# 128 bytes of padding ahead of the weight tiles in a two-layer transformer kernel

## The chip, the cores and the metric

The kernel runs on one core of one Trainium2 chip. The metric is the device time of one execution in microseconds (us); a comparison between two kernels is made on the median of several runs.

## The reference

Two layers work on 512 latent tokens and 256 context tokens, 1024 wide, in fp32. Each layer is a half-step SwiGLU, a token mixing (six GQA heads, a short gated convolution and six MLA heads over one input and one output projection), and another half-step SwiGLU. Every sub-layer is scaled, shifted and gated by vectors made from a conditioning vector. Cut to what matters:

```python
def half_ffn(h, g, shift, scale, gate, wg, wu, wd):
    return h + 0.5 * gate * swiglu(modulate(rms_norm(h, g), shift, scale), wg, wu, wd)

for l in range(2):
    ml, mc = silu(c) @ w_mod[l] + b_mod[l], silu(c_ctx) @ w_mod[l] + b_mod[l]   # nine vectors each
    x, ctx = half_ffn(x, ..., wg[l, 0], wu[l, 0], wd[l, 0]), half_ffn(ctx, ...)
    y_l, y_c = token_mixing(modulate(rms_norm(x, ...)), modulate(rms_norm(ctx, ...)), ...)
    x = x + ml[5] * y_l
    x = half_ffn(x, ..., wg[l, 1], wu[l, 1], wd[l, 1])
    if l == 0:                                       # the context isn't needed after the last mixing
        ctx = half_ffn(ctx + mc[5] * y_c, ...)
return x
```

## The kernel before, in words

**Precision.** A weight or an activation in fp32 is split into a high part (a cast to fp32r on ACT) and a low part (a subtraction on DVE), and a product is three matmuls into the same PSUM tile: high weight by high token, high weight by low token, low weight by high token. Each matmul instruction loads its own stationary operand, 128x128, even where the one before had the same (the profile counts 16,088 weight loads, PEld, beside 16,088 matmuls, PE).

```python
def mm3(wh, wl, rh, rl, spans, first, last):
    for st, mv, f, l in ((wh, rh, first, False), (wh, rl, False, False), (wl, rh, False, last)):
        for view, d in spans:
            te.matmul(out=d, lhsT=st, rhs=view(mv), start=f, stop=l)
```

**Stages.** The feed-forward networks take most of the time. Their first chunks of hidden columns are done as plain products (`classical`); the others by seven half-size products in the manner of Strassen (`Tile.p1` to `Tile.p7`), for which DVE makes sums of weights and of tokens. The hidden columns are then multiplied by blocks of the down weights and added to the residual stream. In the mixing stage the projections use tokens as the moving operand where the output is wanted transposed, and tokens as the stationary operand where it is wanted by token: the projection of GQA inputs (`wn`, 384 and 288 columns) and the two up-projections of MLA (`up`, 288 and 384 columns a step). Attention works through units of two blocks of queries.

**Where the order comes from.** The kernel writes the order of the instructions of TensorE (PE), VectorE (DVE) and ScalarE (ACT) by hand in the long stretches (`chain` and `unchain` tie each instruction behind the one before it on its engine); weights come by DMA, nearly all on SP's queue, a buffer or two ahead.

**Where tiles lie.** A tile in SBUF is a byte address, the same in all 128 partitions, and a length. A pool hands out tiles by tag: the first request for a tag sets aside room for all its buffers behind the room that was handed out before, and later requests for that tag reuse it. So the order of first requests sets the addresses. Behind the constants and the residual stream `xT` come, in this order:

| tag | what is in it | bytes of a buffer x buffers | first address modulo 512 |
|---|---|---|---|
| `s` | slots: tokens, activations, split tokens (high and low), attention operands, sometimes split weights | 3072 x 34 | 320 |
| `t` | temporaries, raw down weights of the second half of each network | 3072 x 5 | 320 |
| (small) | small vectors, a few bytes each | | |
| `st`, `st2` | sums of squares, 216 bytes, set aside as 224 | 224 x 1 each | 384, 96 |
| `mscr` | scratch for the largest temporary, raw up weights (`wu`), raw output weights (`wo`) | 4096 x 1 | 320 |
| `ot` | small outputs of attention | 1024 x 2 | 320 |
| `wr` | raw weights as they land from DMA | 4096 x 2 | 320 |
| `wh`, `wl` | high and low parts of a weight block | 4096 x 3 each | 320 |
| `mr` | raw modulation weights; sums of weights (`ws`); some split weights (`we`, `w`) | 4096 x 2 | 320 |
| `mq` | raw modulation weights; gate weights (`wg`) | 4096 x 1 | 320 |

The two tiles `st` and `st2` are requested at one place in the prologue, ahead of the first tile of `mscr`:

```python
    for tag in ("st", "st2"):
        pool.tile([P, NT, 9], F32, name=nm(tag), tag=tag, bufs=1)
    Rs = pool.tile([P, D], F32, name="Rs", tag="mscr", bufs=1)
```

All sizes between a buffer and the next of these tags, and the steps between the blocks of a weight tile (128 columns of 4 bytes) and between the halves of a token tile (384 or 256 columns), are multiples of 512 bytes. So for nearly every matmul the address of the stationary operand and that of the moving operand differ by a multiple of 512. The exceptions are few: in the MLA up-projection of queries the moving weights go in steps of 288 columns, which is 1152 bytes or 128 modulo 512 (tokens are stationary there), and some matmuls have constants (`ident`, `ones`, `sT`, `s4`) as an operand.

In this text the offset of a matmul is the address of its stationary operand minus that of its moving operand, modulo 512.

Of the kernel before, what the change touches and what calls it, by code (L numbers as in the profile page):

```python
# [8 lines left out]
F32 = mybir.dt.float32  # L9
# [6 lines left out]
P = 128  # L16
# [32 lines left out]
def tile_net(ctx: ExitStack, tc: tile.TileContext, a, out):  # L49
# [37 lines left out]
    pool = ctx.enter_context(tc.tile_pool(name="pool", bufs=1))  # L87
# [4 lines left out]
    def nm(s):  # L92
        uid[0] += 1
        return f"{s}{uid[0]}"
# [1981 lines left out]
    wm0_mm(0, 5, KD)  # L2076
    for tag in ("st", "st2"):
        pool.tile([P, NT, 9], F32, name=nm(tag), tag=tag, bufs=1)
    Rs = pool.tile([P, D], F32, name="Rs", tag="mscr", bufs=1)
    se.copy(Rs[:, LAT], Rl)  # L2080
    wm0_copy(0)
# [162 lines left out]
```

## Time and profile before

| what | number |
|---|---|
| median of 3 runs | 2710.05 us (2707.39 to 2710.4) |
| the profiled execution's own time | 2708.69 us |
| its span, from the first to the last instruction | 2706.8 us |
| PE busy | 2647.6 us, 98% of the span, 16,088 matmuls |
| weight loads (PEld) busy | 2513.8 us, 93% |
| DVE, ACT, POOL busy | 2047.0, 1140.6, 147.3 us |
| mean granted TensorE clock | 0.998 |
| DMA | 266.09 MB moved, mean 98 GB/s |

The prediction's first lines are from the page of the profile. All recorded operations go through one helper line (L67), so groups are told apart by the names of tiles: `ps<-s,wh` is a matmul into a PSUM tile `ps` with a slot and a tile of `wh` as operands. Of a matmul the row gives a modelled duration, from its start to the end of its last result; matmuls overlap, so what a stream of them costs is the distance from start to start, read from the timeline.

### The profile page before, as it was taken

To read this page: it belongs to the slowest core of one execution; us is meant where nothing else is said; L and a number is where in the kernel's file an instruction comes from. 1 tells how busy PE (TensorE), PEld (TensorE's weight loads), DVE (VectorE), ACT (ScalarE), POOL (GpSimd) and SP (SyncE) were. 2 spreads that over 40 slices of the span, in tenths; PEclk is the share of its full clock that TensorE was granted. 3 is DMA by queue.
4 is the path that set the end of the run, shared out by engine and by line. 5 is a ranking of instruction groups with operands and counts; after the bars stand their busy time and mean duration, and the time that the engine had idled before them with its cause. 6 is when DMAs were issued, how large, how long until landed. Compare 5 with 4: busy or idle time off the path is not lost. (4 is left out here: it accounts for less than half of the span.)

```text
span 2706.8 us, 40646 instructions
## 1 busy us (share of the span) xinstructions
PE 2647.6 (98%) x16088; PEld 2513.8 (93%) x16088; DVE 2047.0 (76%) x3493; ACT 1140.6 (42%) x1991; POOL 147.3 (5%) x224
## 2 busy tenths in 40 slices
PE   8999999999999999999999999999999999999999
PEld 5999999989888889999999999999998888889988
DVE  6856777777789987777777777777767798676655
ACT  5223333341478633333334433333343488444433
POOL 0000000000230100000000000000000221001110
PEclk9999999999999999999999999999999999999999
DMA  7313333234100321333333123333325101246544
GB/s 253 117 59 106 105 105 108 84 88 149 36 2 9 110 94 55 108 103 109 109 109 102 59 83 106 109 104 104 101 88 162 49 9 40 92 126 176 148 134 120
DMA packets 102927, 266.09 MB, mean 98 GB/s; under 512 B 12240, under 2 KB 41680, under 8 KB 102736
## 3 DMA queue, kind: packets, MB, share of 16 engines
q1 hardware_dynamic: 96112, 249.33, 27.8%
q0 software_dynamic: 6624, 14.16, 2.6%
q8 instruction: 127, 2.08, 0.3%
q14 instruction: 64, 0.52, 0.1%
HBM read 256.63 MB, written 2.10 MB: 96 GB/s over the span
## 5 line engine op out<-in xcount | busy, mean ns | idle before, releaser
L67 PE MATMUL ps<-s,wh 128*128 128x384 f32 (+2 forms) x4292 | 983.6, 338 | 7.5 <-ACT t L67 3.8
L67 PEld LDWEIGHTS ps<-s,wh 128*128 128x128 f32 x4292 | 742.5, 188 | 51.3 <-issue 5.2
L67 PE MATMUL po<-s,wh 128*128 128x384 f32 (+2 forms) x3164 | 765.2, 327 | 2.9 <-ACT t L67 2.2
L67 PE MATMUL ps<-s,wl 128*128 128x384 f32 (+2 forms) x2146 | 610.4, 337 | 1.3 <-DVE wl L67 1.2
L67 PEld LDWEIGHTS po<-s,wh 128*128 128x128 f32 x3164 | 554.4, 189 | 15.5 <-ACT t L67 3.3
L67 PE MATMUL po<-s,wl 128*128 128x384 f32 (+2 forms) x1582 | 517.2, 327 | 0.0
L67 PEld LDWEIGHTS ps<-s,wl 128*128 128x128 f32 x2146 | 387.3, 188 | 20.1 <-DVE wl L67 3.5
L67 PEld LDWEIGHTS po<-s,wl 128*128 128x128 f32 x1582 | 299.1, 189 | 5.4
L67 DVE SCALAR_TENSOR_TENSOR junk<-mr,sb 128x1024 fp8e4<-128x1024 f32 x224 | 273.7, 1222 | 16.1 <-DMA mr<-in_wm_dram 15.3
L67 DVE TENSOR_TENSOR wl<-wr,wh 128x1024 fp32r<-128x1024 f32 (+3 forms) x179 | 193.1, 1081 | 112.9 <-ACT wh L67 112.7
L67 DVE SCALAR_TENSOR_TENSOR xT<-ps,mod,xT 128x256 f32<-128x256 f32 (+1 forms) x360 | 198.7, 594 | 103.4 <-PE ps L67 101.3
L67 ACT CAST wh<-wr 128x1024 fp32r<-128x1024 f32 (+3 forms) x179 | 165.2, 926 | 202.9 <-PE ps L67 137.7
L67 ACT COPY t<-po 128x384 f32<-128x384 f32 (+2 forms) x215 | 96.9, 451 | 258.9 <-PE po L67 258.5
L67 PE MATMUL po<-s,s 128*128 128x256 f32 (+3 forms) x1216 | 191.9, 309 | 7.3 <-ACT s L67 2.7
L67 PEld LDWEIGHTS po<-s,s 128*128 128x128 f32 x1216 | 173.8, 191 | 14.8 <-ACT s L67 3.4
L67 ACT ACTIVATE t<-t 128x384 f32<-128x384 f32 (+1 forms) x142 | 70.9, 499 | 255.0 <-DVE t L67 255.0
L67 DVE TENSOR_TENSOR t<-po,t 128x384 f32<-128x384 f32 (+2 forms) x223 | 115.7, 524 | 34.2 <-ACT t L67 23.9
L67 DVE TENSOR_TENSOR s<-t,s 128x768 fp32r<-128x768 f32 (+3 forms) x144 | 104.2, 727 | 43.4 <-ACT s L67 42.9
L67 ACT CAST wh<-ws 128x1024 fp32r<-128x1024 f32 x71 | 74.6, 1051 | 147.0 <-PE ps L67 90.6
L67 ACT CAST s<-t 128x768 fp32r<-128x768 f32 (+3 forms) x144 | 92.6, 649 | 102.7 <-DVE t L67 102.5
L67 PE MATMUL po<-s,w 128*128 128x384 f32 x636 | 118.7, 334 | 0.0
L67 ACT CAST wh<-t 128x768 fp32r<-128x768 f32 x80 | 66.7, 837 | 113.6 <-PE ps L67 108.7
(197 smaller groups left out, 3306.7 us busy)
## 6 DMA issues: line engine op xcount, KB each, us to landing
mr<-in_wm_dram SPq DMA_DIRECT2D x128, 512.0 KB, 3.3
wr<-in_wg_dram SPq DMA_DIRECT2D x82, 512.0 KB, 3.3
wu<-in_wu_dram SPq DMA_DIRECT2D x71, 512.0 KB, 3.3
t<-in_wd_dram SPq DMA_DIRECT2D x80, 384.0 KB, 3.6
wr<-in_wiT_dram SPq DMA_DIRECT2D x22, 512.0 KB, 3.6
ws<-in_wu_dram POOLq DMA_DIRECT2D x36, 256.0 KB, 4.3
wr<-in_wu_dram SPq DMA_DIRECT2D x17, 512.0 KB, 3.3
wr<-in_wo_dram SPq DMA_DIRECT2D x14, 512.0 KB, 4.0
```

The source lines that it names most:

```text
L67: f(*args, **kw)
```

## The change

It requests one more tile from the same pool, 32 fp32 values (128 bytes) in each partition, between `st2` and the first tile of `mscr`. Nothing reads or writes it.

```diff
     for tag in ("st", "st2"):
         pool.tile([P, NT, 9], F32, name=nm(tag), tag=tag, bufs=1)
+    pool.tile([P, 32], F32, name="edge", tag="edge", bufs=1)
     Rs = pool.tile([P, D], F32, name="Rs", tag="mscr", bufs=1)
```

The instructions of every engine, their order, shapes and waits are the same in both programs; only the addresses of the tags behind the new tile differ. `mscr`, `ot`, `wr`, `wh`, `wl`, `mr` and `mq`, and the small tiles behind them, go from 320 to 448 modulo 512; slots, temporaries and all that lies ahead stay. By the addresses, the matmuls of the program stand like this (an fp32 matmul that isn't a transpose is counted once here, and twice in the profile's 16,088):

| offset modulo 512 | before | after |
|---|---|---|
| 0 | 14,592 | 1,354 |
| 128 | 0 | 12,636 |
| 384 (the stationary operand 128 bytes behind) | 60 | 662 |
| 256 | 60 | 60 |
| others, with a constant as an operand | 1,190 | 1,190 |

The 1,354 that stay at 0 have both operands in slots.

## Prediction

> **What bounds the kernel now.** I read the page first, for the share of each engine and the clock, then the busy time by stretch, then the timeline of PE and of its weight loads.
>
> ```profile
> span 2706.8 us, 40646 instructions
> PE 2647.6 (98%) x16088; PEld 2513.8 (93%) x16088; DVE 2047.0 (76%) x3493; ACT 1140.6 (42%) x1991; POOL 147.3 (5%) x224
> PEclk9999999999999999999999999999999999999999
> ```
>
> PE is busy for 2647.6 of 2706.8 us, so it waits for 59.2 us in all. The clock is granted throughout. The stage of the seven products, which is typical, shows it more sharply (columns: length, then busy time and count of PE, PEld, DVE, ACT and POOL, then clock, DMA share, GB/s):
>
> ```profile
> 1180.00:1300.00 120.00, 119.84 (x690) 119.26 (x689) 95.60 (x150) 38.45 (x57) 0.00 (x0) 1.00 0.30 99
> 1300.00:1420.00 120.00, 119.84 (x690) 119.26 (x689) 93.71 (x148) 38.41 (x59) 0.00 (x0) 1.00 0.32 105
> ```
>
> 690 matmuls in 120 us are 173.9 ns each, and PE has no gap. So the time of the kernel is the distance from one matmul's start to the next, summed; the change can move it only by that distance, or by making PE wait more than its 59.2 us.
>
> The distance by width, from the timeline of PE (start, length, matmuls in a row), at 384, 512 and 256 columns:
>
> ```profile
> 1240.10 0.33 PE L67 MATMUL po<-s,wl 128*128 128x384 f32 x1
> ...
> 1242.18 0.33 PE L67 MATMUL po<-s,wl 128*128 128x384 f32 x1
> ```
>
> ```profile
> 1002.29 1.52 PE L67 MATMUL po<-s,we 128*128 128x512 f32 x6
> 1003.65 0.62 PE L67 MATMUL po<-s,wh 128*128 128x512 f32 x2
> ```
>
> ```profile
> 1019.98 0.28 PE L67 MATMUL ps<-s,wl 128*128 128x256 f32 x1
> ...
> 1021.78 0.28 PE L67 MATMUL ps<-s,wl 128*128 128x256 f32 x1
> ```
>
> At 384, twelve matmuls (four times two of `wh` and one of `wl`) lie between 1240.10 and 1242.18: 173.3 ns each. At 512, six in 1.36 us: 226.7 ns. At 256, fifteen in 1.80 us: 120.0 ns. The three lie on a line: 53.3 ns for 128 columns, or 0.4167 ns a column, and 13.3 ns that don't depend on the width. That fixed part is the only thing in a matmul that the place of its operands could change. All these matmuls have offset 0.
>
> **The change, part by part.** It adds no instruction, no wait and no transfer, and moves none. It changes addresses. Four things could follow.
>
> (1) PE's two reads. The weight load of the next matmul runs during the present one; they start together (timeline of PEld):
>
> ```profile
> 1240.10 0.36 PEld L67 LDWEIGHTS po<-s,wh 128*128 128x128 f32 x2
> 1240.45 0.19 PEld L67 LDWEIGHTS po<-s,wl 128*128 128x128 f32 x1
> ```
>
> The load at 1240.10 starts with the `wl` matmul of that time. With offset 0, both reads begin at the same place modulo 512; after the change the weights begin 128 bytes on, in 12,636 matmuls. No matmul of the trace has offset 128 with a full weight load, so its price is bounded by two rows.
>
> The nearest is the MLA up-projection of queries. Its moving weights go in steps of 1152 bytes, so the nine matmuls of one pass have offset 0 three times, 384 (which is -128) three times, and 256 three times:
>
> ```profile
> 735.16 1.36 PE L67 MATMUL ps<-we,s 128*128 128x288 f32 x9
> 736.36 0.29 PE L67 MATMUL ps<-wh,s 128*128 128x288 f32 x1
> ```
>
> Nine take 1.20 us, 133.3 ns each. The line through the offset-0 widths gives 120.0 + 32 x 0.4167 = 133.3 ns. So 128 bytes between the reads, in the other direction, and 256, cost nothing that shows. The row is rounded to 0.01 us, which over the six matmuls off 0 leaves 1.7 ns either way: 12,636 x 1.7 = 21 us as the bound of a loss or gain by this row.
>
> The other bounds what could be won. In the prologue, matmuls of 256 columns load four columns of weights instead of 128 (`128*4`), at changing offsets:
>
> ```profile
> 31.85 2.04 PE L67 MATMUL ps<-s,s 128*4 128x256 f32 x16
> 37.08 2.04 PE L67 MATMUL ps<-s,s 128*4 128x256 f32 x16
> ...
> 49.13 2.03 PE L67 MATMUL ps<-s,s 128*4 128x256 f32 x16
> ```
>
> (2.04 - 0.28) / 15 = 117.3 ns, with 0.28 the length of a single 256-column matmul in the rows above. So of the 13.3 ns, 10.6 are there with hardly any weights read; reading 128 columns beside the stream adds 2.7 ns at most. If the shift took all of that away from 12,636 matmuls, 34 us would go. I take 0 for this term: the up-projection is nearest in width of the load, in engine and in distance, and lies on the line. The ends -34 and +34 are kept for the rivals, and 21 us for the range.
>
> Here the Trainium skill, "TensorE: Matmul & The Clock Gate", section "Part 2: What happens when you issue a matmul", has a rule that speaks against any effect: PE has two independent SBUF read ports, and loading the next weights doesn't take read bandwidth from the running matmul. By that rule the term is exactly 0, though the four-column row shows 2.7 ns between a small and a full load, which the rule doesn't foresee.
>
> (2) DVE's two reads. Two groups change their relation, and the trace has both relations for each (last numbers: busy us, mean ns):
>
> ```profile
> L67 DVE SCALAR_TENSOR_TENSOR junk<-mr,sb 128x1024 fp8e4<-128x1024 f32 x224 | 273.7, 1222 | 16.1 <-DMA mr<-in_wm_dram 15.3
> L67 DVE TENSOR_TENSOR wl<-wr,wh 128x1024 fp32r<-128x1024 f32 x129 | 159.4, 1238 | 102.8 <-ACT wh L67 102.7
> L67 DVE TENSOR_TENSOR wl<-ws,wh 128x1024 fp32r<-128x1024 f32 x71 | 86.9, 1224 | 14.0 <-ACT wh L67 9.5
> L67 DVE TENSOR_TENSOR wl<-t,wh 128x768 fp32r<-128x768 f32 x80 | 76.4, 955 | 24.1 <-ACT wh L67 24.1
> L67 DVE TENSOR_TENSOR s<-t,s 128x768 fp32r<-128x768 f32 x61 | 58.0, 957 | 19.8 <-ACT s L67 19.5
> ```
>
> The modulation product reads `mr` (320) and `sb` (448 by its address): 128 apart now, 0 apart after. It takes 1222 ns; splits of the same width with both inputs at 320 take 1224 and 1238. The split of down weights reads `t` and `wh`, 0 apart now and 128 after; at 0 it takes 955, like the other split of 768. So 0 within about 1%: at most 224 x 16 ns = 3.6 us of DVE's time, and DVE has 24% of the span free.
>
> (3) ACT casts, and (4) the landing of DMAs at 448 instead of 320. No row isolates either. What hides a change of some per cent in them is that PE, in the stretches above, waits for neither: 0.16 us of 120 is idle, ACT is 32% busy there and the DMA engines 30%. If that cover went, a late `wh` would show as a wait of PE for `ACT wh`; a tenth more on ACT's 38.45 us in such a stretch, all of it on PE's path, would cost 3.8 us in 120. I take 0.
>
> Sum: 2708.69 us (the profiled execution's own time, 1.9 over its span) + 0 + 0 + 0 = 2708.7. The median of the runs is 1.4 us higher, within their spread of 3 us. I predict 2709.
>
> **The rivals.**
>
> Faster: the two reads that start together at one place hold each other up, and the 2.7 ns are that. A shift of 128 keeps them apart, and 12,636 x 2.7 = 34 us go: 2675. For it: the difference between loads of 4 and 128 columns. Against it: the six matmuls at 384 and 256 would have been 2.7 ns shorter each, 16 ns in a row that should then read 1.18, and it reads 1.20. It decides from 0.43 ns a matmul on (5.4 us, 0.2%). A part of it, up to 1.7 ns, would give 2688 to 2703.
>
> A far end of the same: the section "Back-to-back issue gap" of "TensorE: Matmul & The Clock Gate" in the Trainium skill gives N/2.4 + 2.5 ns for warm matmuls, 109 ns at 256 columns where the trace has 120.0. Were that whole excess of 10.8 ns a collision of reads, an estimate by the page would be 136 us less, 2573. The four-column row keeps 117.3 ns with 1/32 of the weights, so I give it 2 in 100.
>
> Slower: the place where both start together is the good one. A matmul of 256 columns reads its operand in 107 ns (256 x 0.4167) while the load reads half as many columns. Started level, the moving read is ahead at once and stays ahead within the first 512 bytes; started 128 bytes behind, it must overtake the weights in mid-stream and holds up there. The mechanism is in the matmul after each weight load, its price that of one such hold-up, for which I take the same 2.7 ns: 34 us, 2743. For it: the fixed 13.3 ns is so even at offset 0 that nothing there can be colliding, so there is more to lose than to win. Against it: at 384 and 256 the reads meet too, one lap on, and cost nothing. It decides from the same 0.43 ns.
>
> The change doesn't do what it says: 1,354 matmuls with both operands in slots stay at 0, so a tenth of any gain or loss is missing; the time stays 2709 if the effect is nought, and it is part of the first case.
>
> **How the numbers follow.** 0.2% of 2709 is 5.4 us, 0.43 ns for each of 12,636 matmuls; about that much can be told from no change here. The rows exclude 2.7 ns in the same place only at other offsets, and exclude 0.43 ns nowhere. No change: 0.58. Faster: 0.20, of it 0.09 with a part up to 1.7 ns, 0.09 with the full 34 us, 0.02 with more. Slower: 0.22, half up to 21 us, half at 34 or more. The range takes the bound of the up-projection's row on both sides, 2709 - 21 and 2709 + 21, and so holds 0.58 + 0.09 + 0.11 = 0.78; rounded outward to 2686 and 2733 it holds 8 in 10. The range of the likeliest case alone is 2704 to 2714.
>
> **What would show it.** In the profile after, the twelve matmuls of the 1240 stretch should again lie 2.08 us apart from first to last, the stretch from 1180 to 1300 should again count 690, and the 256-column rows 120.0 ns. Right is also that the nine of the up-projection, now at 384, 256 and 128, take 1.20 us again. For the faster rival these distances shrink: 170.6 ns at 384 columns, 703 matmuls in 120 us. For the slower one they grow to 176, 682 in 120 us. If the distances are the same and the time isn't, the rows of PE's waits must have grown beyond 59 us, and term (3) or (4) is wrong. The prediction is wrong if offset 128 is unlike 384 and 256, which no row of this trace can exclude.

## The result, and the profile after

The changed kernel takes 2731.22 us (median; 2728.14 to 2735.5), the kernel before 2710.23 beside it: a ratio of 1.0085, interval 1.007 to 1.0101. The padding makes the kernel 21 us slower.

The page and the busy time by stretch, after (columns as before):

```profile
span 2730.8 us, 40646 instructions
PE 2671.9 (98%) x16088; PEld 2532.7 (93%) x16088; DVE 2047.0 (75%) x3493; ACT 1142.2 (42%) x1991; POOL 147.4 (5%) x224
...
1180.00:1300.00 120.00, 119.99 (x682) 119.43 (x682) 91.33 (x144) 38.38 (x58) 0.00 (x0) 1.00 0.29 99
```

The span grew by 24.0 us and PE's busy time by 24.3; PE's idle time is 58.9 us where it was 59.2. DVE, ACT and POOL are busy for as long as before. So PE waits no more in all: it does the same matmuls, with 682 in the 120 us that held 690. One wait did grow, that for casts of `wh` on ACT, from 0.2 to 2.9 us; others shrank by as much. The timeline of PE, at 384, 512, 256 and 288 columns:

```profile
1249.81 0.51 PE L67 MATMUL po<-s,wh 128*128 128x384 f32 x2
...
1251.92 0.51 PE L67 MATMUL po<-s,wh 128*128 128x384 f32 x2
```

```profile
1012.52 1.56 PE L67 MATMUL po<-s,we 128*128 128x512 f32 x6
1013.92 0.63 PE L67 MATMUL po<-s,wh 128*128 128x512 f32 x2
```

```profile
1029.76 0.28 PE L67 MATMUL ps<-s,wl 128*128 128x256 f32 x1
...
1031.54 0.28 PE L67 MATMUL ps<-s,wl 128*128 128x256 f32 x1
```

```profile
742.95 1.36 PE L67 MATMUL ps<-we,s 128*128 128x288 f32 x9
744.15 0.29 PE L67 MATMUL ps<-wh,s 128*128 128x288 f32 x1
```

Twelve matmuls of 384 columns take 2.11 us, 175.8 ns each (173.3 before); six of 512 take 1.40, 233.3 each (226.7); fifteen of 256 take 1.78, 118.7 each (120.0); the nine of the up-projection, 1.20 as before. So the effect has a size and even a sign that depend on the width of the stream. Matching every matmul of the two traces and adding the differences from start to start, those of 384 columns that went from offset 0 to 128 (7,899) give +17.6 us, those of 512 (1,974) +10.8, of which 6.2 is 3.2 ns each in the streams and the rest in waits between them, those of 256 (2,600) -2.1, and all others -2.4: the 24.0 us of the span.

The starts in the 1240 stretch show that this isn't a fixed price either. In nanoseconds from start to start, taken from the trace:

```
before: 173 173 174 173 173 174 173 173 174 ...
after:  175 178 174 175 178 174 175 177 174 ...
```

Before, every matmul of this stretch costs the same 173.3. After, they repeat in a rhythm of three (elsewhere of five, with single distances up to 182).

### The profile page after: what moved, and what is told of

Its sections match the earlier page's. It is cut to its first block, busy times and chain, and to the rows that moved or that the text cites. A ratio compares the mean times of both kernels' runs of the same rounds, so it can differ in the third digit from the quotient of the medians.

```text
span 2730.8 us, 40646 instructions
## 1 busy us (share of the span) xinstructions
PE 2671.9 (98%) x16088; PEld 2532.7 (93%) x16088; DVE 2047.0 (75%) x3493; ACT 1142.2 (42%) x1991; POOL 147.4 (5%) x224
## 5 line engine op out<-in xcount | busy, mean ns | idle before, releaser
L67 PE MATMUL ps<-s,wh 128*128 128x384 f32 (+2 forms) x4292 | 994.4, 341 | 9.1 <-ACT t L67 3.8
L67 DVE SCALAR_TENSOR_TENSOR junk<-mr,sb 128x1024 fp8e4<-128x1024 f32 x224 | 273.4, 1220 | 15.2 <-DMA mr<-in_wm_dram 14.3
```

The lines of the kernel that those rows point to most:

```text
L67: f(*args, **kw)
```

## The experiments

Two theories were left. A: the cost lies in PE's two reads and depends on the offset between them. B: it comes from where the weight tiles lie by themselves, through the other engines or DMA.

**A sweep of offsets with nothing but matmuls (e1_sweep).** It has three moving tiles and one tile of weight blocks; the chains differ in width and in where the stationary operand starts:

```python
for w in (256, 288, 320, 384, 448, 512):
    for o in range(16):
        for i in range(48):
            c = 128 * (i % 8) + 8 * o                # 32 bytes further with each o
            nc.tensor.matmul(out=acc[:, 0:w], lhsT=wt[:, c:c + 128], rhs=mv[i % 3][:, 0:w], ...)
```

> This kernel leaves out the network: it runs only chains of 48 matmuls, with 128 columns of weights loaded for each, at widths 256, 288, 320, 384, 448 and 512 and at offsets (stationary minus moving address, modulo 512) of 0, 32, ... 480; DVE, ACT and DMA are idle meanwhile. Theory A, the cost lies in PE's two reads and depends on the offset: at offset 0 the matmuls stand 120.0, 133.3, 173.3 and 226.7 ns apart at 256, 288, 384 and 512 columns, and at offset 128 they stand 176 ns apart at 384 and 232 at 512, as in the changed kernel, with nothing added at 256 and 288. Theory B, the cost comes from where the weight tiles lie by themselves, through the other engines or DMA: 173.3 and 226.7 at every offset.

The letter behind the `o` of a row is the offset: `oa` 0, `oe` 128, `og` 192, `oi` 256. From the start of a row to the next start are 48 matmuls.

```profile
125.61 6.57 PE L43 MATMUL oe<-mv,wt 128*128 128x288 f32 x48
132.02 6.48 PE L43 MATMUL of<-mv,wt 128*128 128x288 f32 x48
...
314.70 8.49 PE L43 MATMUL oa<-mv,wt 128*128 128x384 f32 x48
323.03 8.49 PE L43 MATMUL ob<-mv,wt 128*128 128x384 f32 x48
...
348.21 8.62 PE L43 MATMUL oe<-mv,wt 128*128 128x384 f32 x48
356.67 8.64 PE L43 MATMUL of<-mv,wt 128*128 128x384 f32 x48
365.15 8.48 PE L43 MATMUL og<-mv,wt 128*128 128x384 f32 x48
373.47 8.64 PE L43 MATMUL oh<-mv,wt 128*128 128x384 f32 x48
...
605.47 11.09 PE L43 MATMUL oa<-mv,wt 128*128 128x512 f32 x48
616.40 11.35 PE L43 MATMUL ob<-mv,wt 128*128 128x512 f32 x48
...
650.02 11.32 PE L43 MATMUL oe<-mv,wt 128*128 128x512 f32 x48
661.18 11.37 PE L43 MATMUL of<-mv,wt 128*128 128x512 f32 x48
...
694.57 11.05 PE L43 MATMUL oi<-mv,wt 128*128 128x512 f32 x48
705.46 11.35 PE L43 MATMUL oj<-mv,wt 128*128 128x512 f32 x48
```

At 384 columns: 8.33 us at offset 0 (173.5 ns), 8.46 at 128 (176.3), 8.32 at 192 (173.3). At 512: 10.93 at 0, 11.16 at 128 (232.5), 10.89 at 256 (226.9). At 288 columns and offset 128: 133.5. In ns, without the first two matmuls of each chain (at offset 0 the chain of 512 columns takes longer to settle: its last thirty stand 226.7 apart):

| offset | 256 | 288 | 320 | 384 | 448 | 512 |
|---|---|---|---|---|---|---|
| 0 | (start of the run) | 131.7 | 146.6 | 173.4 | 202.7 | 227.4 |
| 32 | 118.3 | 133.3 | 146.6 | 173.3 | 204.4 | 233.4 |
| 64 | 117.8 | 133.2 | 146.7 | 174.7 | 202.2 | 233.4 |
| 96 | 117.3 | 133.3 | 146.7 | 176.6 | 200.0 | 234.4 |
| 128 | 118.6 | 133.4 | 146.7 | 176.0 | 204.0 | 232.5 |
| 160 | 119.8 | 131.7 | 146.7 | 176.6 | 205.3 | 233.3 |
| 192 | 117.8 | 132.2 | 146.6 | 173.4 | 200.0 | 228.9 |
| 224 | 117.8 | 133.4 | 146.7 | 176.6 | 206.7 | 233.3 |
| 256 | 119.8 | 131.7 | 146.7 | 173.5 | 206.7 | 226.7 |

From 256 to 480 the rows repeat those from 0 to 224, but for 448 columns at offset 0: the period is 256 bytes, not 512. The changed kernel's 176 and 232 come out of chains with no other engine at work. That is theory A, with its numbers at 384 and 512 columns. At 256 and 320 columns no offset costs more than a multiple of 256 does; at 288, which was expected to lose nothing, offset 0 has 131.7 and 128 has 133.4. Nor is 0 the best everywhere: at 448 columns it has 202.7 and 256 has 206.7, where 96 and 192 have 200.0.

**Both moved together (e2_both128).** The same padding at the head of the pool, so that tokens and weights both lie at 448:

```diff
+    pool.tile([P, 32], F32, name="edge", tag="edge", bufs=1)
     chain("te", "ve", "se")
     stl, stc = Stats(LAT, D), Stats(CTXS, D, ps)
```

> The same 128 bytes, but ahead of the slots: tokens and weights both move from 320 to 448, so the offset is 0 again and the weights lie exactly where the changed kernel has them. Theory A: as before, 2710 us, ratio 1.000. Theory B: as the changed kernel, 2731, ratio 1.0085.

**Two other distances (e3_rel384, e4_rel256).** e3 takes `st2` out of the loop and puts 96 bytes of padding behind `st`; e4 has the change with twice the padding:

```diff
-    for tag in ("st", "st2"):
+    for tag in ("st",):                                                        # e3
         pool.tile([P, NT, 9], F32, name=nm(tag), tag=tag, bufs=1)
+    pool.tile([P, 24], F32, name="edge", tag="edge", bufs=1)                   # e3
+    pool.tile([P, 64], F32, name="edge", tag="edge", bufs=1)                   # e4, with the loop as it was
```

> Weights 128 bytes behind the tokens modulo 512 (offset 384). Theory A if any distance between the two reads costs: 2731 or about, ratio 1.008. Theory A if only a load that lies ahead of the stream costs (the moving read overtakes it): 2710, ratio 1.000, as the few matmuls at 384 in the trace of before had it. Theory B (place of the weights, now 192): no number; anything but 2710 would need a rule of its own.

> Weights 256 bytes ahead (offset 256, half a period). Theory A if any distance costs: 2731 or more. Theory A with overtaking: the stream has to run 256 bytes further before it meets the load; at 384 and 512 columns it does, so slower than before, between 2715 and 2735. If 128 alone is bad: 2710.

Measured: e2 1.000 (0.9987 to 1.0014), e3 1.0072 (1.0054 to 1.0091), e4 0.9996 (0.9984 to 1.0007). The stretch from 1180 to 1300 in each, in this order:

```profile
1180.00:1300.00 120.00, 119.84 (x690) 119.26 (x689) 95.27 (x148) 38.20 (x58) 0.00 (x0) 1.00 0.31 101
```

```profile
1180.00:1300.00 120.00, 120.00 (x682) 119.44 (x681) 91.92 (x145) 37.83 (x56) 0.00 (x0) 1.00 0.30 97
```

```profile
1180.00:1300.00 120.00, 119.84 (x691) 119.26 (x690) 95.65 (x149) 38.45 (x57) 0.00 (x0) 1.00 0.30 98
```

690, 682 and 691 matmuls. e2 has the weights where the changed kernel has them and is as fast as before: theory B is out. e3 and the changed kernel, which are 256 apart, cost the same, and so do e4 and the kernel before: the period of 256 holds in the kernel. e3 and the changed kernel together also rule out a cost that falls only on a load ahead of the stream, or only on one behind it.

**The cost taken apart (e5_sweep2), and two more distances in the kernel (e6_rel96, e7_rel192).** e6 and e7 drop `st` and `st2` there, so that they come behind the weights, and pad 32 and 128 bytes:

```diff
-    for tag in ("st", "st2"):
-        pool.tile([P, NT, 9], F32, name=nm(tag), tag=tag, bufs=1)
+    pool.tile([P, 8], F32, name="edge", tag="edge", bufs=1)                    # e6; 32 in e7, 24 in e9
```

The second sweep has the chains of the first with these runs, written in short (width, columns loaded, start of the stationary operand in elements):

```python
for w in (384, 512): runs += [(w, 128, 4 * j) for j in range(16)]                             # fp32r, steps of 16 bytes
for cols in (96, 64, 32): for w in (384, 512): runs += [(w, cols, 8 * j) for j in range(8)]   # fewer columns loaded
for w in (256, 384, 512): runs += [(w, 128, 8 * j) for j in range(16)]                        # bf16, steps of 16 bytes
runs += [(384, 128, 24 if i % 4 == 0 else 0), (512, 128, 24 if i % 4 == 0 else 0)]            # one load in four is off
```

> Leaves out the network, as the first sweep, and splits the cost of an offset: fp32r at 384 and 512 columns in steps of 16 bytes from 0 to 240; fewer loaded columns (96, 64, 32) at offsets 0 to 224; bf16 operands at 256, 384 and 512 columns; and chains in which one load in four lies 96 bytes ahead. If the two reads disturb each other in SBUF by place, the period of 256 bytes is a matter of bytes: in bf16 it is again 256 bytes or the effect is gone, since a load then covers 256 bytes only; fewer loaded columns shorten the overlap and lower the cost in proportion; and the chains with one load in four off cost a quarter of the 3.3 and 7.6 ns at offset 96, or less. If the offset costs by some rhythm of the whole chain (each matmul's start set by the one before), one load in four costs anything but a quarter, and the steps of 16 bytes are uneven.

In fp32r at 384 columns the steps of 16 bytes are uneven: 173.3 ns at 16, 32, 48 and 64, 176.1 at 80, 173.3 at 96 and 112, 176.0 at 128, 177.3 at 144, 176.6 at 160, 173.3 at 176 and 192, 175.5 at 208. Two of these, 64 and 96, had 174.7 and 176.6 in the first sweep. Fewer loaded columns don't lower the cost in proportion. At 384 columns the mean of eight offsets is 174.5 ns with a full load and 174.4 to 174.6 with 96, 64 or 32 columns; at 512 it goes from 232.1 to 230.9 with 96 and 230.0 with 64, and then up to 232.8 with 32. With 32, the eight offsets give 173.3 to 176.7 at 384 and 230.3 to 240.0 at 512, so that 0, the best place for a full load at 512, costs 231.4. One load in four off by 96 bytes makes a chain of 512 columns 233.3 ns a matmul, 6.6 more, where a quarter of 7.6 is 1.9; one of 384 columns has 175.0, 1.7 more, where a quarter of 3.3 is 0.8. The proportions that a collision by place was expected to have are refuted. And in bf16 it is gone. Sixteen offsets from `ods` to `oeh`, then 512 columns:

```profile
872.36 7.96 PE L57 MATMUL ods<-mb,wb 128*128 128x384 bf16 x48
...
989.36 7.96 PE L57 MATMUL oeh<-mb,wb 128*128 128x384 bf16 x48
997.16 10.52 PE L57 MATMUL oei<-mb,wb 128*128 128x512 bf16 x48
1007.52 10.52 PE L57 MATMUL oej<-mb,wb 128*128 128x512 bf16 x48
```

From `ods` to `oeh` fifteen chains take 117.00 us. Every chain takes 7.80 us at 384 columns and 10.36 at 512: 162.5 and 215.8 ns, whatever the offset. In fp32r the best is 173.3 and 226.7.

> The whole kernel with weights 96 bytes ahead (offset 96). By the first sweep, against offset 0: 7899 matmuls of 384 columns by +3.2 ns, 1974 of 512 by +7.6 ns, 2600 of 256 by -2.5 ns: 25.3 + 15.0 - 6.5 = 34 us, 2744, ratio 1.0125. A theory in which any offset that isn't a multiple of 256 costs the same gives the 2731 of offset 128.

> The whole kernel with weights 192 bytes ahead (offset 192). By the first sweep: 384 columns 0, 512 by +2.1 ns x 1974 = +4.1 us, 256 by -2.0 ns x 2600 = -5.2 us: 1 us less than before, which is no difference, ratio 0.9996. A theory in which any offset that isn't a multiple of 256 costs gives 2731, ratio 1.008.

Measured: e7 0.9997 (0.9984 to 1.0009), as the sweep said. e6 1.001 (0.9998 to 1.0023) where 1.0125 was expected: a clear miss. Its stretch counts 690 matmuls:

```profile
1180.00:1300.00 120.00, 119.84 (x690) 119.26 (x689) 95.67 (x149) 39.36 (x58) 0.00 (x0) 1.00 0.29 96
```

At offset 96 the kernel's matmuls of 384 columns stand 173.3 apart, as in the second sweep, and not 176.6, as in the first. Those of 512 did slow down (8.0 us in all) and those of 256 got faster (-5.4 us). So one offset can have two prices. I formed a theory for that: each matmul's start is set by the one before, a chain settles into a repeating rhythm, and at some offsets several rhythms hold.

**Many starts (e8_phase).**

```python
nc.tensor.matmul(out=acc[:, 0:160 + 24 * pre], ...)      # pre = 0 to 7: another phase for the chain behind it
for i in range(32): ...                                  # the chain, 384 or 512 columns, one offset
```

> Leaves out the network: chains of 32 matmuls at 384 and 512 columns, at offsets 0, 64, 96, 128, 160 and 192, each offset eight times, and each time behind one matmul of another width (160 to 328 columns), so that the chain starts at another phase. Theory R (a chain falls into a repeating rhythm, and at some offsets several rhythms hold, which the start decides): at 64 and 96 bytes and 384 columns some chains settle at 173.3 ns and others at 174.7 or 176.6; at 0 all settle at 173.3; at 128 and 160 none does. Theory F (a fixed price for each offset, and the two sweeps differ by something else): all eight chains of an offset alike.

Three chains of 384 columns at offset 96 (the second number is the length of 32 matmuls):

```profile
118.38 5.71 PE L47 MATMUL oat<-mv,wt 128*128 128x384 f32 x32
124.05 5.71 PE L47 MATMUL oau<-mv,wt 128*128 128x384 f32 x32
129.73 5.82 PE L47 MATMUL oav<-mv,wt 128*128 128x384 f32 x32
```

The third is 0.11 us longer, 3.5 ns a matmul. Settled, in ns: at 96, seven of eight chains stand at 173.3 and one at 176.7 (174 and 179 in turn); at 64, one at 173.3, four at 174.7, three at 176.7; at 128, all at 175.6 or 176.0; at 160, all at 176.7; at 192, all at 173.3; at 0, all at 173.3 but the chain that is the first work of the run. At 512 columns the eight starts of an offset lie within 1.4 ns. Theory R stands, and theory F falls: the offset decides which rhythms hold, the start which of them a chain falls into.

**A distance where no even rhythm was seen (e9_rel160).** As e6, with 96 bytes of padding.

> The whole kernel with weights 160 bytes ahead. Both sweeps give 176.6 ns at 384 columns and 233.4 at 512 for this offset, so if the price of an offset holds wherever the sweeps agree: 7899 x 3.3 + 1974 x 6.7 = 26 + 13 = 39 us more, 2749, ratio 1.0145, and the slowest of all. If an even rhythm of 173.3 can hold here too (Theory R with other starts), 2711 to 2725.

1.0116 (1.0089 to 1.0144), 2740.73 us beside 2710.66, 679 matmuls in the stretch:

```profile
1180.00:1300.00 120.00, 120.00 (x679) 119.48 (x678) 90.85 (x142) 37.26 (x56) 0.00 (x0) 1.00 0.30 98
```

It is the slowest offset that was tried in the kernel, 30 us and not the 39 expected: 384 columns cost 23.4 us more (26 expected), and 512 7.2 (13 expected), perhaps because chains of 512 are short in the kernel and mixed with others, which no run tests.

No kernel here is faster than the one before by more than a measurement can tell; by their medians 0, 96, 192 and 256 are equally good within 0.2%, and 128, 160 and 384 are worse.

## Why the prediction was wrong

The step that failed is term (1), PE's two reads, taken as 0. It came to 24 us of the span: +17.6 at 384 columns, +10.8 at 512 and -2.1 at 256. Its row was the up-projection of queries, "nearest in width of the load, in engine and in distance". It is right as a row: its nine matmuls take 1.20 us after the change too, as foretold. But it is 288 columns wide, and the first sweep has 131.7 to 133.4 ns at that width for every offset. The load's width was matched; the stream's width wasn't, and it decides: 384 and 512 columns, two thirds of the matmuls, had no row off offset 0. Besides, of the row's three offsets, 256 is the same as 0, because the period is 256; only three of nine matmuls tested anything.

Nor were those three shown to be free. The row was held against a line through 256, 384 and 512 columns, which gives 133.3 ns at 288. But the trace of before has matmuls of 288 columns at offset 0, the projection of GQA inputs (`po<-s,s`, both operands in slots). They stand 131.7 apart (mean of the 263 distances below 150 ns) in rhythms such as 127, 133, 134, 133, and the sweep has 131.7 there too. So the row lay on the line and above the price of its own width, and the part that doesn't depend on the width wasn't fixed even at offset 0.

The bound on a loss or gain from that row, 1.7 ns on 12,636 matmuls, has the size about right by accident: it spread over all widths what lies on two of them (+2.2 ns on 384, +5.5 on 512, -0.8 on 256, waits included).

The second bound, 2.7 ns between loads of 4 and 128 columns, was for what could be won at 256 columns, and there it holds: 117.3 at offset 96, the four-column row's number. The rivals took it as the price at every width, and that failed: at 512 columns an offset costs up to 7.7 ns, and with loads of 32 columns the second sweep loses as much and more.

The slower rival had the sign, the place and the sight of it: 176 ns at 384 columns and 682 matmuls in 120 us, both as measured. Its price, 34 us, was too high mainly since it charged the 256-column matmuls too; it was also too high at 384 and too low at 512. Its mechanism, the moving read overtaking the load in mid-stream, isn't shown, and e3 speaks against it: there the load lies 128 bytes behind, with nothing to overtake at the start, and the kernel is as slow. Its argument, that there was more to lose than to win, held at 384 and 512 columns, where no offset came below 173.3 and 226.7; at 256 there was something to win. Its ground, that all is even at offset 0, doesn't hold for the 288 columns of the trace of before.

Terms (2) to (4) were right within what shows: DVE and ACT are busy for as long as before (2047.0 both times; 1142.2 beside 1140.6), the modulation product takes 1220 ns where it took 1222, and PE waits no more in all, though 2.7 us more for casts of `wh`, the sign named for terms (3) and (4). For the split of down weights the old trace had no row 128 apart, against what term (2) says: both rows of 768 columns are at 0. After the change it takes 955 ns as before.

The Trainium skill ("TensorE: Matmul & The Clock Gate", section "Part 2: What happens when you issue a matmul") has it that loading the next weights takes no read bandwidth from the running matmul. The bf16 chains agree: 109.2, 162.5 and 215.8 ns at all sixteen offsets of each width. These are also the N/2.4 + 2.5 ns that the Trainium skill gives for warm matmuls ("TensorE: Matmul & The Clock Gate", section "Back-to-back issue gap"). The fp32r chains don't agree: they stand at least 10.8 ns further apart at 384 and 512 columns, and the place of the load changes it. The measurement decides, and the far rival that read the whole 10.8 ns as a collision which an offset could clear is out: no offset brought 384 columns below 173.3.

What stays open is what the two reads do to each other in fp32r. That the cost hangs on where one operand lies against the other, that it has a period of 256 bytes and that a chain settles into rhythms is shown; why an offset has the rhythms that it has isn't, nor what in bf16 takes the effect away, since both operands changed their type there.

## What to carry to other kernels

In fp32r on a kernel that PE bounds, a small allocation can move the time by 1%. For streams of 384 and 512 columns, keep weights and moving tiles a multiple of 256 bytes apart; other widths have other best places (at 448 columns 96 and 192), so measure them. After any change to small tiles look at the distance from start to start in a long stream before looking for a reason elsewhere. When a row of the old trace is to stand for a new case, match it in everything that could matter, the width of the stream too, and count how many of its instances really differ. A price from an isolated sweep needs several starts: a chain that depends on its own past can have more than one.

## What the runs showed of the hardware that I had not expected

- In fp32r, matmuls of 384 columns stand 173.3 ns apart at best and 512 columns 226.7, in bf16 162.5 and 215.8: 10.8 and 10.9 ns more for each matmul in fp32r.
- The offset between the stationary and the moving operand adds up to 4.0 ns at 384 columns (177.3 at 144 bytes) and 7.7 at 512 (234.4 at 96) with a full load, with a period of 256 bytes. 256 columns are 2.5 ns faster at 96 bytes than at 256, and 448 columns 2.7 ns or more faster at 96 than at 0.
- PE's stream of loads and matmuls settles into an even distance or into rhythms of two, three, four, five or seven matmuls (174 and 179 in turn at 96 bytes and 384 columns; 235, 233, 232, 237, 238, 231, 234 at 96 bytes and 512), and at 64 bytes and 384 columns three of them hold, at 173.3, 174.7 and 176.7 ns.
